# A first norm completed ahead of the projections, whose products are convolved and gated from PSUM in pairs of banks

## The chip, the cores and the metric

One NeuronCore of a Trainium2 chip runs one program. The metric is the device time of one execution in microseconds. TensorE (PE) multiplies matrices into PSUM, eight banks of 512 float32 columns on 128 partitions. The DVE (VectorE) and ACT (ScalarE) read PSUM and SBUF, POOL (GpSimd) reads SBUF alone. DMAs are issued by SP's queue. Each engine works off its own list in order and waits on semaphores for the others.

## The reference, cut to what matters

The model has two layers, a Hyena mixer and a differential attention. The change lies in the first of them:

```python
y = rmsnorm(h, norm_pre[i])                     # y = h * rsqrt(mean(h*h) + 1e-6) * g
u = y @ w_in + b_in                             # 1024 -> 8192
streams = dwconv_centred(u[..., :3 * D_INNER], conv_w, conv_b)   # 3 taps along the tokens
x0, x1, v = jnp.split(streams, 3, axis=-1)
z = u[..., 3 * D_INNER:]
h_fwd, h_bwd = hyena_filters(T, ...)            # a small sine network over the positions
v = bidir_long_conv(v * x1, h_fwd, h_bwd, skip) # by FFT in the reference
y = v * x0
return (y * jax.nn.silu(z)) @ w_out
```

There are T = 528 tokens (16 meta tokens and 512), 1024 channels and 2048 inner channels.

## The kernel before

Everything is held transposed, channels on partitions and the 528 tokens along the free axis, so x is eight slabs of 128 x 528. For float32 accuracy each operand of a large matmul is split into a rounded high part and the rest (`hi` on ACT, line 209, and `lo`, line 212), and a product takes three matmuls: high by high, high by rest, rest by high (`project`, line 396). One output tile of a projection, 128 channels by 528 tokens, is 8 slabs x 3 products x 2 halves of 264 tokens, 48 matmuls, done in two steps of 24 (slabs 0 to 3, slabs 4 to 7).

There are 64 such tiles in Hyena: for each of eight chunks two tiles each of v, x, y and z (`in_items`, `in_tile`). The matmuls of the tiles are filler: a `Filler` holds them as a list of steps, each with a cost in microseconds, and the code of the stages asks it to put so many microseconds of steps between its own instructions (`run`, `upto`). `fetch` loads a weight tile and splits it. A scheduler then orders each engine's list by a simulated time line, with the order of the program as priority; an instruction can be given a higher priority (`high_priority`), a fixed order (`keep_in_program_order`), or an edge behind another on the same engine (`issue_after`).

In the kernel before, `first_load` loads x slab by slab, multiplies by the gain and splits it, and sums the squares on the DVE (line 511), while the projections begin at once with the gained but not yet normed x. `first_norm` takes the column sums by six matmuls (line 270), computes 1/rms by the DVE (`rsqrt`), and spreads it over the partitions into `rb0` (line 286, line 525). Since the norm is a factor of each token, it is applied when a product leaves PSUM: `scaled` in `in_tile` (line 554) multiplies each half, one bank, by `rb0` on the DVE into SBUF (`u`, or `cv` for z). From there a three-tap convolution is made of one ACT step (line 569, middle tap and bias) and two DVE steps (lines 570 and 571). GpSimd writes minus the bias into the two edge columns of `u` (line 566) so that the bias vanishes at the ends. For z, ACT takes silu (line 559).

The eight banks of PSUM are two pools: `psB` with five single banks and `psP` with three. Projected tiles take two banks of `psP` (one tile takes them from `psB`), as do the transforms of the filter's taps (`tap_transform`, lines 753 to 760); the output projection (`out_tile`, line 918) takes two banks of `psB`, each half added to the accumulator by the DVE (line 925).

The order of the stages: the sine network (`filter_net`, three layers, line 637) and the tables run with the first four tiles and four more steps, then `filters` makes the taps of eight chunks and transforms them with filler between, then eight times `long_conv` with the tiles of the next chunk and the output tiles of the last as filler, then `boundary` (second norm) and the attention. In `taps` the first product's row 0 is multiplied by one half (line 720).

## Time and profile before

| | |
|---|---|
| median of 3 runs | 1425.76 us (1424.94 to 1428.54) |
| the profiled execution | 1427.81 us |
| its span, first to last instruction | 1426.0 us |
| TensorE busy | 1339.9 us, 94% |
| DVE, ACT, GpSimd busy | 1094.9, 740.5, 569.0 us |
| mean granted TensorE clock | 0.977 |
| Hyena's share of the span | until about 705 us |

The profile is one execution on the chip. It has a page with sums, and a trace that can be asked for any stretch: busy times by window, instructions in order of time, what each idle time of an engine ended with. A row that ends with `[6.48 <-DVE sqk L280]` says that the engine stood idle for 6.48 us before it and that the DVE's instruction of line 280 on tile sqk ended that. TensorE's matmuls are pipelined and overlap in their rows; the distance of their starts tells their rate. One float32 matmul with a single column has two records. A few per cent of the matmul records can be missing.

### The profile page before, as it was taken

The page shows a single profiled execution, that of the slowest core. Times are in us where ns is not written, and L with a number is a line of the kernel's source. Part 1 is how long each engine was busy: PE and PEld are TensorE (multiplying, and loading weights), DVE is VectorE, ACT ScalarE, POOL GpSimd, SP SyncE. Part 2 cuts the span into 40 slices and gives each one's busy share as a digit, 9 for nine tenths or more (in the row PEclk, how much of TensorE's full clock was granted, in tenths as well). Part 3 has the DMA queues.
Part 4 walks back from the last instruction along what each step waited for, and adds up shares of the span by engine and source line. Part 5 has one row for each costly group of instructions (what it writes and reads, how often), then busy time and mean ns, then how long its engine had stood idle before and what let it go on. Part 6 is the DMA issues. An engine that isn't in the chain of part 4 may idle for free. (4 is left out here: it accounts for less than half of the span.)

```text
span 1426.0 us, 25213 instructions
## 1 busy us (share of the span) xinstructions
PE 1339.9 (94%) x9296; PEld 1245.4 (87%) x9296; DVE 1094.9 (77%) x1979; ACT 740.5 (52%) x1415; POOL 569.0 (40%) x671
## 2 busy tenths in 40 slices
PE   5889999999999999999989899999999999999995
PEld 4789889889899999999889788898898989898884
DVE  8889988888988888888877765675656676675677
ACT  5345533453535353534344767666555556666543
POOL 6266634432333323242432234434333343434325
PEclk9899999999999999999979899999999999999998
DMA  6244342668978686877431322323332231322341
GB/s 203 93 140 156 137 152 90 205 231 269 315 241 300 216 288 219 287 239 259 148 110 40 117 89 89 108 85 119 118 117 106 76 132 46 145 92 111 125 157 59
DMA packets 104171, 222.10 MB, mean 156 GB/s; under 512 B 11808, under 2 KB 16160, under 8 KB 104048
## 3 DMA queue, kind: packets, MB, share of 16 engines
q1 hardware_dynamic: 104048, 220.49, 44.6%
q8 instruction: 73, 1.20, 0.3%
q14 instruction: 50, 0.41, 0.1%
HBM read 158.58 MB, written 61.87 MB: 155 GB/s over the span
## 5 line engine op out<-in xcount | busy, mean ns | idle before, releaser
L396 PE MATMUL b<-xh,wh 128*128 128x264 f32 x1024 | 268.3, 293 | 13.9 <-DVE u L554 10.9
L396 PE MATMUL b<-xl,wh 128*128 128x264 f32 x1024 | 264.8, 290 | 2.6 <-DVE xl L506 2.6
L396 PE MATMUL b<-xh,wl 128*128 128x264 f32 x1024 | 262.2, 290 | 1.1 <-POOL wl L212 1.1
L396 PEld LDWEIGHTS b<-xh,wh 128*128 128x128 f32 x1024 | 185.3, 194 | 19.6 <-DVE u L554 13.7
L396 PEld LDWEIGHTS b<-xl,wh 128*128 128x128 f32 x1024 | 184.7, 194 | 4.8 <-DVE xl L506 3.5
L209 ACT CAST wh<-wr 128x512 fp32r<-128x512 f32 x220 | 129.7, 618 | 109.0 <-DMA wr<-in_w_in 33.9
L396 PEld LDWEIGHTS b<-xh,wl 128*128 128x128 f32 x1024 | 183.4, 193 | 1.9 <-POOL wl L212 1.4
L212 POOL TENSOR_TENSOR wl<-wr,wh 128x512 fp32r<-128x512 f32 x64 | 90.9, 1441 | 103.0 <-ACT wh L209 102.8
L212 DVE TENSOR_TENSOR wl<-wr,wh 128x512 fp32r<-128x512 f32 x156 | 123.5, 818 | 10.1 <-ACT wh L209 9.7
L353 ACT CAST ah<-ar 128x512 fp32r<-128x512 f32 x94 | 56.7, 617 | 88.2 <-DMA ar<-in_w_z 29.6
L1382 DVE TENSOR_REDUCE mx<-a 128x1 f32<-128x528 f32 x128 | 89.0, 697 | 15.2 <-PE a L1379 15.1
L393 PE MATMUL b<-xh,wh 128*128 128x512 f32 x232 | 92.8, 400 | 4.4 <-DVE acc L1325 4.4
L393 PE MATMUL b<-xl,wh 128*128 128x512 f32 x232 | 91.9, 396 | 0.0
L212 DVE TENSOR_TENSOR pl<-b,ph 128x512 fp32r<-128x512 f32 x64 | 43.9, 688 | 62.4 <-ACT ph L209 62.4
L393 PE MATMUL b<-xh,wl 128*128 128x512 f32 x232 | 91.7, 395 | 0.0
L566 POOL TENSOR_SCALAR u<-vecs 128x1 f32<-128x1 f32 x96 | 42.4, 460 | 123.5 <-DVE cv L571 73.6
L354 DVE TENSOR_TENSOR al<-ar,ah 128x512 fp32r<-128x512 f32 x94 | 70.1, 755 | 26.9 <-ACT ah L353 26.1
L1388 POOL COPY pp<-pp 128x80 f32<-128x80 f32 x64 | 20.8, 325 | 145.6 <-DVE pp L1387 105.0
L1325 DVE SCALAR_TENSOR_TENSOR acc<-b,rh,acc 128x512 f32<-128x512 f32 x96 | 70.4, 743 | 10.6 <-PE b L1310 10.4
L1262 PE MATMUL b<-wh,xh 128*128 128x256 f32 x256 | 74.1, 289 | 0.4 <-DVE vl L1272 0.4
L1262 PE MATMUL b<-wl,xh 128*128 128x256 f32 x256 | 73.0, 285 | 0.0
L1262 PE MATMUL b<-wh,xl 128*128 128x256 f32 x256 | 72.8, 284 | 0.0
(391 smaller groups left out, 4101.3 us busy)
## 6 DMA issues: line engine op xcount, KB each, us to landing
wr<-in_w_in SPq DMA_DIRECT2D x128, 256.0 KB, 3.8
hsp<-ho SPq DMA_DIRECT2D x16, 512.0 KB, 2.6
ar<-in_w_v SPq DMA_DIRECT2D x32, 256.0 KB, 4.2
wr<-in_w_out SPq DMA_DIRECT2D x32, 256.0 KB, 3.7
H<-hsp SPq DMA_DIRECT2D x16, 512.0 KB, 4.7
w_v_h<-ah SPq DMA_DIRECT2D x32, 256.0 KB, 3.3
w_v_l<-al SPq DMA_DIRECT2D x32, 256.0 KB, 3.4
ar<-in_w_out SPq DMA_DIRECT2D x32, 256.0 KB, 4.0
```

Of the source, the lines that this page charges most:

```text
L209: self.nc.scalar.copy(dst, src)
L212: (eng or self.nc.vector).tensor_tensor(dst, src, hi.bitcast(F32), op=ALU.subtract)
L353: keep(nc.scalar.copy(h, raw))
L354: keep(nc.vector.tensor_tensor(l, raw, h.bitcast(F32), op=ALU.subtract))
L393: te.matmul(ps, w[:, wk], x[:, k, first:T], start=st, stop=sp)
L396: te.matmul(ps[h], w[:, wk], x[:, k, h * TH:(h + 1) * TH], start=st, stop=sp)
L566: g.tensor_scalar(u[:, e:e + 1], b_in[:, mt:mt + 1], -1.0, None, op0=ALU.mult)
L1262: te.matmul(ps[:n, :256], x, wv[k // 4][w][:, wk], start=(k == 0 and q == 0), stop=(k == KT - 1 and q == len(ops) - 1))
L1325: self.nc.vector.scalar_tensor_tensor(y, ps, r, y, op0=ALU.mult, op1=ALU.add)
L1382: v.tensor_reduce(mx, ps[:, :, :TH], axis=AX.XY, op=ALU.max, negate=True)
L1388: self.nc.gpsimd.tensor_copy(view(p, 0, [META, 5], [1, META]), view(p, MR - META, [0, 5], [1, META]))
```

## The change

It completes the norm before the projections. `first_load` loads all of x first, with the network's table behind slab 1 and the vectors behind slab 5, then the first two weight tiles. Squares are summed by TensorE: six one-column matmuls a slab. `first_norm` has a shorter root (a power on GpSimd and one Newton step on the DVE), makes the row factors by six small matmuls (`rows`) and then multiplies each slab by gain and factor on the DVE, casts it on ACT and subtracts on the DVE, at high priority and in a fixed order. What follows on ACT and DVE is put behind the last slab.

`in_tile` no longer scales. ACT reads a pair of banks and writes the middle tap with bias into a padded buffer `cv` (six fixed ones), the DVE adds the left and right taps from the pair, shifted by writing at another offset, and GpSimd adds an edge correction to two columns, computed once. Silu of z is read from the pair as well. PSUM becomes `psB` with four single banks and `psP` with two pairs; output tiles take pairs, too, and are evacuated by one instruction. Items 1 and 2 of the first chunk's steps are exchanged, one layer of the network runs ahead of the norm instead of two, and with two steps after each later layer ten steps are asked for before the filters instead of eight. The factor one half goes into the constant `hbas`.

```diff
--- before.py
+++ after.py
...
     hbas = np.stack([np.cos(sg), np.sin(sg)]).transpose(3, 0, 1, 2, 4)
+    hbas[0, 0, 0, 0] *= 0.5
...
         px = ExitStack()
-        self.psB = px.enter_context(tc.tile_pool(name="ps0", bufs=5, space=PSUM))
-        self.psP = px.enter_context(tc.tile_pool(name="ps1", bufs=3, space=PSUM))
+        self.psB = px.enter_context(tc.tile_pool(name="ps0", bufs=4, space=PSUM))
+        self.psP = px.enter_context(tc.tile_pool(name="ps1", bufs=2, space=PSUM))
         with ExitStack() as cx:
...
             cb2 = self.tl(k0, [P, 48], F32, "cb2")
-            self.rb0 = self.tl(k0, [P, T], F32, "rb0")
+            edge = self.edge = self.tl(k0, [P, 48, 2], F32, "edge")
+            self.cv = [self.tl(pa, [P, T + 2], F32, f"cv{i}", bufs=1) for i in range(6)]
+            self.cv_at = 0
+            for t in self.cv:
+                g.memset(view(t, 0, [T + 1, 2]), 0.0)
...
             items += vx(0)
+            items[1], items[2] = items[2], items[1]
             for c in range(NCH):
...
                 with tc.tile_pool(name="pf", bufs=1) as pf:
-                    net = self.net_load(pf)
-                    part = self.first_load(pf, fill)
-                    self.load(dtl, I["dtail"])
+                    xts, sums, net = self.first_load(pf, fill)
+                    layers = self.filter_net(pf, hs, net)
+                    next(layers)
+                    with tc.high_priority(offset=400):
+                        last = self.first_norm(pf, xts, sums)
                     g.tensor_tensor(cb2, cw[:, 0], cw[:, 1], op=ALU.add)
...
                     g.tensor_tensor(cb2, cb2, cb, op=ALU.add)
-                    layers = self.filter_net(pf, hs, net)
-                    for _ in (0, 1):
-                        next(layers)
-                    self.first_norm(pf, self.rb0, part)
-                    fill.fetch(2, g)
-                    fill.upto(4)
-                    for _ in layers:
-                        fill.upto(fill.at + 2)
-                    self.tables(pf, vb, nb, ib, hb)
+                    for i in (0, 1):
+                        g.tensor_tensor(edge[:, :, i], cw[:, 2 * i], b_in[:, 0:48], op=ALU.mult)
+                    g.tensor_scalar(edge, edge, -1.0, None, op0=ALU.mult)
+                    self.load(dtl, I["dtail"])
+                    with tc.issue_after(last[0]), tc.issue_after(last[1]):
+                        fill.upto(4)
+                        for _ in layers:
+                            fill.upto(fill.at + 2)
+                        self.tables(pf, vb, nb, ib, hb)
                 self.filters(fpool("pl"), hs, hb, dtl, rnt, dpf, dpb, hsp, lambda us: fill.run(us, first[1]))
...
         nc = self.nc
-        part = []
+        sums = self.tl(self.psB, [P, 512], F32, "b")
+        xts = []
         for k in range(KT):
...
             self.load(xt, self.I["xT"][:, k])
-            if k == 0:
+            xts.append(xt)
+            if k == 1:
+                net = self.net_load(pf)
+            if k == 5:
                 self.load(self.vecs, self.I["vecs"])
-                fill.fetch(0, nc.gpsimd)
-            gain = self.gains[:, 0, k:k + 1]
-            nc.scalar.activation(self.xh[:, k], xt, AF.Copy, scale=gain)
-            nc.vector.scalar_tensor_tensor(self.xl[:, k], xt, gain, self.xh[:, k].bitcast(F32), op0=ALU.mult,
-                                           op1=ALU.subtract)
+        for i in (0, 1):
+            fill.fetch(i, nc.vector)
+        for k, xt in enumerate(xts):
             sq = self.tl(pf, [P, T], F32, "sqk", bufs=4)
             nc.scalar.activation(sq, xt, AF.Square)
-            if part:
-                nc.vector.tensor_tensor(part[0], part[0], sq, op=ALU.add)
-            else:
-                part.append(sq)
-            if k == 3:
-                fill.fetch(1, nc.gpsimd)
-        return part
-
-    def first_norm(self, pf, rb, part):
-
-        r = self.token_rms(part, [(j * 88, j * 88 + 88) for j in range(6)])
-        dg = self.diagonals(r, 0, 6, 88, self.tl(pf, [P, T], F32, "sqk", bufs=4))
+            for j in range(6):
+                nc.tensor.matmul(sums[:88, j:j + 1], sq[:, j * 88:j * 88 + 88], self.ones[:, 0:1],
+                                 start=k == 0 and j == 0, stop=k == KT - 1 and j == 5)
+        return xts, sums, net
+
+    def first_norm(self, pf, xts, sums):
+
+        v, s, m = self.nc.vector, self.nc.scalar, 88
+        a, y, q, r = [self.tl(self.small, [P, 8], F32, t)[:m, :6] for t in ("rs_a", "rs_y", "rs_q", "rms")]
+        v.tensor_scalar(a, sums[:m, 0:6], 1.0 / D, 1e-6, op0=ALU.mult, op1=ALU.add)
+        self.nc.gpsimd.tensor_tensor(y, a, self.mhalf[:m, :6], op=ALU.pow)
+        v.scalar_tensor_tensor(q, y, -0.5, y, op0=ALU.mult, op1=ALU.mult)
+        v.tensor_tensor(q, q, a, op=ALU.mult)
+        v.scalar_tensor_tensor(r, q, 1.5, y, op0=ALU.add, op1=ALU.mult)
+        rb = self.tl(pf, [P, T], F32, "rb0")
         for h in (0, 1):
             ps = self.tl(self.psB, [P, 512], F32, "b")
-            self.spread(dg[:, h * TH:(h + 1) * TH], ps[:, :TH])
-            self.nc.scalar.copy(rb[:, h * TH:(h + 1) * TH], ps[:, :TH])
+            self.rows(r, 3 * h, 3, m, ps[:, :TH])
+            s.copy(rb[:, h * TH:(h + 1) * TH], ps[:, :TH])
+        keep = self.tc.keep_in_program_order
+        for k in range(KT + 1):
+            if k < KT:
+                xt, xh = xts[k], self.xh[:, k]
+                keep(v.scalar_tensor_tensor(xt, xt, self.gains[:, 0, k:k + 1], rb, op0=ALU.mult, op1=ALU.mult))
+                cast = keep(s.copy(xh, xt))
+            if k:
+                low = keep(v.tensor_tensor(self.xl[:, k - 1], xts[k - 1], self.xh[:, k - 1].bitcast(F32), op=ALU.subtract))
+        return cast.ins, low.ins
...
         if part == 0:
-            res["ps"] = [self.tl(self.psB if (c, idx) == (0, 1) else self.psP, [P, 512], F32, "b")[:, :TH] for _ in (0, 1)]
-        ps = res["ps"]
-        self.project(ps, wt, 0, part)
+            res["ps", idx] = self.tl(self.psP, [P, 2, 512], F32, "b")
+        ps = res["ps", idx][:, :, :TH]
+        self.project((ps[:, 0], ps[:, 1]), wt, 0, part)
         if part == 0:
             return
-        r2 = lambda t: t.rearrange("p (h t) -> p h t", h=2)
-
-        def scaled(dst):
-            for h in (0, 1):
-                sl = slice(h * TH, (h + 1) * TH)
-                v.tensor_tensor(dst[:, sl], ps[h], self.rb0[:, sl], op=ALU.mult)
-
+        cv = self.cv[self.cv_at % 6]
+        self.cv_at += 1
+        at = lambda o: view(cv, o, [TH, 2], [1, TH])
+        y = cv[:, 1:T + 1]
         if kind == "z":
-            z = self.tl(pa, [P, T], F32, "cv", bufs=4)
-            scaled(z)
-            s.activation(z, z, AF.Silu, bias=b_in[:, mt:mt + 1])
+            s.activation(at(1), ps, AF.Silu, bias=b_in[:, mt:mt + 1])
             gt = self.tl(pa, [P, T], F32, "G", bufs=2)
-            g.tensor_tensor(gt, res["y", i], z, op=ALU.mult)
+            g.tensor_tensor(gt, res["y", i], y, op=ALU.mult)
             res["G", i] = gt
             return
-        u = self.tl(pa, [P, T + 2], F32, "u", bufs=2)
-        for e in (0, T + 1):
-            g.tensor_scalar(u[:, e:e + 1], b_in[:, mt:mt + 1], -1.0, None, op0=ALU.mult)
-        scaled(u[:, 1:T + 1])
-        y = self.tl(pa, [P, T], F32, "cv", bufs=4)
-        s.activation(y, u[:, 1:T + 1], AF.Identity, bias=cb2[:, mt:mt + 1], scale=cw[:, 1, mt:mt + 1])
-        v.scalar_tensor_tensor(y, u[:, 0:T], cw[:, 0, mt:mt + 1], y, op0=ALU.mult, op1=ALU.add)
-        v.scalar_tensor_tensor(y, u[:, 2:T + 2], cw[:, 2, mt:mt + 1], y, op0=ALU.mult, op1=ALU.add)
+        s.activation(at(1), ps, AF.Identity, bias=cb2[:, mt:mt + 1], scale=cw[:, 1, mt:mt + 1])
+        for o in (2, 0):
+            v.scalar_tensor_tensor(at(o), ps, cw[:, 2 - o, mt:mt + 1], at(o), op0=ALU.mult, op1=ALU.add)
+        ends = view(cv, 1, [T - 1, 2])
+        g.tensor_tensor(ends, ends, self.edge[:, mt], op=ALU.add)
         res[kind, i] = y
...
                 v.tensor_tensor(pm[0:1, 0], pm[0:1, 0], pm[0:1, 1], op=ALU.add)
-                v.tensor_scalar(pm[0:1, 0], pm[0:1, 0], 0.5, None, op0=ALU.mult)
             else:
...
         ho = self.tl(ph, [P, 4, 256], F32, "ho", bufs=2)
-        ps = [self.tl(self.psP, [P, 512], F32, "b") for _ in (0, 1)]
+        ps = self.tl(self.psP, [P, 2, 512], F32, "b")
         for a in (0, 1):
...
                     for (bh, mh) in ((0, 0), (0, 1), (1, 0)):
-                        nc.tensor.matmul(ps[par][:, a * 256:(a + 1) * 256],
+                        nc.tensor.matmul(ps[:, par, a * 256:(a + 1) * 256],
                                          hb[a][bh][:, par, st, jt * P:(jt + 1) * P],
...
                         i += 1
-        pv = lambda q: ps[q].rearrange("p (a b) -> p a b", a=2)
+        pv = lambda q: ps[:, q].rearrange("p (a b) -> p a b", a=2)
         s.copy(ho[:, 0::2], pv(0))
...
         gs = st["g"]
-        pss = [self.tl(self.psB, [P, 512], F32, "b")[:, :TH] for _ in (0, 1)]
+        pair = self.tl(self.psP, [P, 2, 512], F32, "b")[:, :, :TH]
+        pss = [pair[:, h] for h in (0, 1)]
         sls = [slice(0, TH), slice(TH, T)]
...
                                      start=(i == 0 and q == 0), stop=(i == 1 and q == 2))
-        for ps, sl in zip(pss, sls):
-            ya = self.yacc[:, dt, sl]
-            if c == 0:
-                nc.scalar.copy(ya, ps)
-            else:
-                nc.vector.tensor_tensor(ya, ya, ps, op=ALU.add)
+        ya = self.yacc[:, dt].rearrange("p (h t) -> p h t", h=2)
+        if c == 0:
+            nc.scalar.copy(ya, pair)
+        else:
+            nc.vector.tensor_tensor(ya, ya, pair, op=ALU.add)
         if dt in (2, 6):
...
         for k in range(KT):
-            tag, bufs = ("cv", 4) if k < 4 else ("u", 2) if k < 6 else ("G", 2)
-            xt = self.tl(pa, [P, T], F32, tag, bufs=bufs)
+            xt = self.cv[(self.cv_at + k) % 6][:, :T] if k < 6 else self.tl(pa, [P, T], F32, "G", bufs=2)
             self.load(xt, I["xT"][:, k])
...
```

## Rows read from the trace of the kernel before

**Rows 1.** page, part 1: busy us, share of the span, instructions

```profile
PE 1339.9 (94%) x9296; PEld 1245.4 (87%) x9296; DVE 1094.9 (77%) x1979; ACT 740.5 (52%) x1415; POOL 569.0 (40%) x671
```

**Rows 2.** busy time by window: length, then PE, PEld, DVE, ACT, POOL; PEclk, DMA share, GB/s

```profile
0.00:60.00 60.00, 38.95 (x196) 34.32 (x197) 48.10 (x74) 28.06 (x44) 31.08 (x34) 0.86 0.45 154
60.00:100.00 40.00, 34.95 (x258) 33.83 (x257) 32.64 (x52) 20.66 (x35) 23.45 (x25) 0.91 0.38 123
100.00:200.00 100.00, 92.19 (x717) 88.45 (x716) 91.68 (x143) 49.02 (x92) 63.63 (x61) 1.00 0.44 154
200.00:705.00 505.00, 490.19 (x3775) 475.79 (x3774) 435.74 (x852) 224.71 (x387) 170.90 (x187) 1.00 0.70 234
```

**Rows 3.** timeline of TensorE: start us, us, line, tiles, count, idle before

```profile
29.88 1.92 PE L270 MATMUL b<-ones,sqk 128*88 128x1 f32 x12 [5.17 <-DVE sqk L511]
...
43.03 2.13 PE L286 MATMUL b<-sqk,ones 88*128 88x264 f32 x4 [6.48 <-DVE sqk L280]
...
45.40 0.64 PE L396 MATMUL b<-xl,wh 128*128 128x264 f32 x2
45.84 0.64 PE L396 MATMUL b<-xh,wl 128*128 128x264 f32 x2
...
82.90 0.79 PE L753 MATMUL b<-pm,hb0h 128*128 128x256 f32 x2 [4.83 <-ACT pm L209]
```

**Rows 4.** the projections' line alone by window: PE and PEld busy (count), PEclk, DMA, GB/s

```profile
0.00:45.00 45.00, 17.64 (x73) 15.80 (x74) 0.86 0.54 184
45.00:60.00 15.00, 13.99 (x96) 13.77 (x96) 0.84 0.18 64
60.00:74.70 14.70, 14.70 (x122) 14.51 (x120) 1.00 0.46 149
```

**Rows 5.** waits of TensorE, 100 to 705 us: total us, times, longest

```profile
PE b L396 <- DVE u L554: 10.9, 10, 2.9
...
PE b L753 <- DVE u L554: 3.5, 3, 1.3
...
PE b L753 <- ACT acc L209: 1.9, 1, 1.9
...
PE b L918 <- DVE acc L925: 0.6, 2, 0.4
```

**Rows 6.** single lines, whole span: count, ns min/median/max, first and last start

```profile
L509 ACT ACTIVATE sqk<-xt x8: 626/642/643, 4.6 to 21.1; 128x528 f32<-128x528 f32 x8
...
L506 DVE SCALAR_TENSOR_TENSOR xl<-xt,vecs,xh x8: 751/760/1782, 7.1 to 20.8; 128x528 fp32r<-128x528 f32 x8
...
L511 DVE TENSOR_TENSOR sqk<-sqk,sqk x7: 690/1304/2861, 11.2 to 28.5; 128x528 f32<-128x528 f32 x7
...
L1454 POOL TENSOR_TENSOR rh<-vv,mhalf x15: 1017/1020/1050, 856.1 to 1394.0; 128x4 f32<-128x4 f32 x15
...
L554 DVE TENSOR_TENSOR u<-b,rb x96: 373/422/436, 44.7 to 691.7; 128x264 f32<-128x264 f32 x96
...
L569 ACT ACTIVATE cv<-u,cb,vecs x48: 815/829/840, 46.1 to 692.8; 128x528 f32<-128x528 f32 x48
...
L720 DVE TENSOR_SCALAR pm<-pm x8: 282/1182/1275, 81.0 to 187.0; 1x256 f32<-1x256 f32 x8
...
L1325 DVE SCALAR_TENSOR_TENSOR acc<-b,rh,acc x96: 730/742/751, 912.5 to 1370.4; 128x512 f32<-128x512 f32 x96
```

**Rows 7.** network's last layer among groups of TensorE, 0 to 60 us: busy us, mean ns

```profile
L637 PE MATMUL b<-hd,net 64*128 64x264 f32 x4 | 1.2, 408 | 0.0
```

**Rows 8.** timeline of the DVE: two convolution chains, first and last of eleven

```profile
143.63 0.76 DVE L554 TENSOR_TENSOR u<-b,rb 128x264 f32<-128x264 f32 x2
...
150.58 0.75 DVE L571 SCALAR_TENSOR_TENSOR cv<-u,vecs,cv 128x528 f32<-128x528 f32 x1
...
398.27 0.76 DVE L554 TENSOR_TENSOR u<-b,rb 128x264 f32<-128x264 f32 x2
...
404.43 0.75 DVE L571 SCALAR_TENSOR_TENSOR cv<-u,vecs,cv 128x528 f32<-128x528 f32 x1
```

4 lines of the change are left out of this document (2 added, 2 removed).

## The prediction

> **What bounds the kernel now.** I read the engine part of the page first: TensorE is busy 94% of the span [rows 1]. Then the busy time by stage: it is above 97% busy from 200 us to 705 us, but only 39 of 60 us at the beginning, 35 of 40 after that and 92 of 100 in the third stage [rows 2]. So up to 705 us TensorE stands still for 21.0, 5.1, 7.8 and 14.8 us, 48.7 us in all. The change touches nothing behind 705 us but the tiles into which the boundary loads x, so a gain can come from these 48.7 us and from matmuls that run at TensorE's lower level (1.2 GHz), and from nowhere else.
>
> The timeline of the beginning tells where they lie [rows 3]. Six column sums start at 29.88 after 5.17 us of waiting for the DVE's sum of squares; the row factors follow at 43.03, after 6.48 us more; only then can projected tiles leave PSUM. After that wait the projections run at 0.22 us each (two in 0.44 us, from 45.40 to 45.84), against 122 in 14.7 us, 0.1205 us each, at granted clock 1.00 [rows 4]. By 60 us 73 + 96 = 169 projection matmuls are recorded [rows 4], seven steps of 24. The last wait of the beginning is at 82.90: the first tap transform waits 4.83 us for the rounded taps [rows 3].
>
> From 100 us on the waits by releaser say what is left: 10.9 us of projections and 3.5 us of tap transforms wait for the DVE scaling of L554, which empties one of the three shared banks [rows 5].
>
> **Start.** Removed: eight DVE adds of squares, the ACT rounding with gain, the scaling of each product. Added: 48 column-sum matmuls instead of 6, a power on GpSimd, six row matmuls for two, and per slab of x one DVE multiply, an ACT cast, a DVE subtraction, all before the first projection. The first square starts at 4.6 us and takes 0.64 us [rows 6], so sums start at 5.2. Six sums take 1.92 us [rows 3]: eight sets take 15.4 us if all run at the lower level, and they end at 20.6; if the clock rises on the way, and x arrives as fast as the sums run, they could end at 15. I take 18. From there: the power takes 1.02 us [rows 6], with the four small DVE steps and the hand-offs I estimate 2.2 us (at least 1.0, the power alone; at most 11.2, what lies between the end of the present sums and 43.03 [rows 3], where the DVE works on the filter network in between). The row matmuls are nearest to L286 and L270, some 2 us [rows 3]; a copy of half a row is about half of L569's 0.83, 0.5 with its hand-off; the first slab then needs 0.76 (L506) and 0.64 us (L509) [rows 6]. The first projection starts at T0 = 18 + 2.2 + 2.0 + 0.5 + 1.4 = 24.1, bounds 21 and 28.
>
> After T0 the DVE sets the pace: 0.76 + 0.69 us (L506, L511) less their overlap, about 1.35 us a slab [rows 6], 10.7 us for eight. The exchanged order of items 1 and 2 lets two tiles use slabs 0 to 3 first: 24 matmuls at 0.22 are 5.3 us, the next 24, in part at the higher level, 3.5; the third step waits for slab 7 and ends at about T0 + 11.8, the fourth at T0 + 14.7. Three more steps at 2.9 us and two filter layers at 1.2 us (L637 [rows 7]) make seven steps at T0 + 25.7 = 49.8 where the kernel before has them at 60. That is -10.2 us, bounds -13.3 and -6.3.
>
> The fetches of the first two weight tiles are moved behind all of x on SP's queue; their halves are needed at T0 only, 14 us later. The network's table moves behind two slabs, a DMA that the sums do not need. The new ordering edges put the third tile's cast, its subtractions and filter layers 2 and 3 behind the last slab on ACT and DVE. The projections wait for that tile at T0 + 14.7; the DVE is free at T0 + 10.7 and needs two subtractions, so it is hidden with 2.6 us to spare. Without that cover every microsecond counts.
>
> **Start of the taps.** L720 goes (the factor one half moves into a constant): 1.18 us at the median, eight times [rows 6], on the chain before 82.90. And five tiles instead of four are asked for before the filters begin, so more projections stand ready while the taps are rounded. The 4.83 us [rows 3] could go altogether, with the 2.3 us that a restart at the lower level costs (96 projections and a layer take 15 us from 45 to 60 [rows 4], 12.7 at the higher level): -7.1; or nothing is gained, if the network, now late on the DVE, makes the taps late. I take -3.2: L720's 1.2 and 2.0 of the remaining 3.6, since hidden and not hidden seem equally likely.
>
> **Emptying PSUM.** Each v, x or y tile loses two scalings of 0.42 us (L554: 96 + 32 times, 54 us of DVE in all), and its ACT and DVE steps read PSUM instead. The trace shows no dearer read there: a three-operand step of 512 columns from PSUM takes 0.742 us (L1325), of 528 from SBUF 0.760 (L506) [rows 6], 1.449 and 1.439 ns a column. The Trainium skill, VectorE: DVE Perf Modes, § Rules for kernel authors, says to copy a matmul's output to SBUF first if many operations will read it. By these rows the copy would cost 0.84 us a tile and win nothing in the operations themselves.
>
> What is lost is the early release. Today a bank is free after its scaling; afterwards the pair is held until the last of three steps. I followed all 48 such tiles from the start of the second scaling (0.34 us behind the first, where one row holds both) to the end of L571: eleven took longer than the 48 x 0.1205 = 5.8 us that the next tile covers, the first 7.4 us (from 143.97), the last 6.6 (from 398.61) [rows 8], together 18 us too long. Less the scaling itself 13.7 us. Against that, two pairs instead of three banks let a whole tile run while the other is emptied. So the 14.4 us of L554 [rows 5] go, and 0 to 14 come; I take 6, as the freed DVE shortens the queue and long-convolution matmuls often lie between. Net -8.4, bounds -14.4 and -0.4.
>
> **Smaller terms.** One tile less of projections is left to cover the transforms. At the end of that stage the transforms wait 1.9 us for rounded taps [rows 5]; I add as much, +1.9, bounds 0 and 5.8 (a whole uncovered tile). Output tiles take turns on two pairs with the projections; 12 matmuls cover 1.45 us, the add on the DVE remains the same work. Two waits of 0.3 us are there now [rows 5]: +1, bounds 0 and 12 (all 40 such tiles wait 0.3). GpSimd loses 96 small writes (L566), for which no wait of TensorE stands in [rows 5], and gets 48 edge sums, ahead of its own products: nothing, bounds -1 and +1. The boundary's loads go to the oldest tiles: nothing, same bounds.
>
> **Sum.** -10.2 - 3.2 - 8.4 + 1.9 + 1.0 = -18.9 us. Against the profiled execution (1427.8 us, span 1426.0) that gives 1408.9; the median of the three runs shown is 1425.8, 2 us less, which would give 1406.9. I say 1408.
>
> **Rivals.** *The norm stays as slow as now*: the chain from the sums to the factors takes its 11 us again because DVE steps of layer 1 and of the first weight tiles lie between. T0 becomes 18 + 11.2 + 2.0 + 0.5 + 1.4 = 33, the start gains 1 instead of 10, and 1427.8 - 18.9 + 9 = 1418. For it: exactly this happened between 31.8 and 43.03. Against it: priority 400, and no big GpSimd work beside it (L511, which now runs beside GpSimd's subtractions, takes between 0.69 and 2.86 us [rows 6]).
>
> *New waits equal the old ones*: the wait for a scaling becomes a wait for the convolution, 14 us instead of 6, and output tiles cost 4: 1427.8 - 18.9 + 8 + 3 = 1420.
>
> *The pair is held too long (slower)*: the convolution's two DVE steps stay at the end of a full DVE queue, as in the eleven chains, but for three quarters of the 48 tiles, and each exceeds its cover by the eleven's mean, 18.3/11 - 0.42 = 1.24 us: 36 x 1.24 = 45 us, instead of the 6 in the sum: 1448. It becomes slower than before from 25 us of such waits on, 20 tiles. The Trainium skill, PSUM — Partial Sum Buffer, § Summary: rules for kernel authors, speaks for this one: evacuate promptly. No row shows a pair held so; the eleven chains show that it is possible, the 37 others that it is not the rule.
>
> *It doesn't do what it says*: the scheduler puts the projections ahead of the norm as it likes. Data dependence excludes it: the first matmul reads the normed slab.
>
> **Chances.** Forecast 0.72, slow norm 0.11, waits that merely change their name 0.10, held pairs 0.07. A measurement here can tell about 0.3%, 4.3 us, from no change: 1421.5 is the bound. The forecast and about half of the second and third (their spread is some 5 us) are faster: 0.82; the rest of these 0.11 within; slower 0.07. Range: the forecast's own ends, all bounds together, are 1392 and above 1420; leaving one in ten on each side I give 1393 to 1424.
>
> **What would show it.** Right: the first projection between 21 and 28 us and no gap over 2 us after it up to 60; fewer than 7 us of TensorE waits on the convolution's DVE line; DVE busy about 50 us less. Wrong: TensorE waits for the second convolution step for over 20 us; sums that end after 22 us; a gap before the first transform as long as now or longer.

## The result, and the profile after

The changed kernel takes 1435.84 us (median of 4 runs, 1435.44 to 1438.92), beside 1425.96 us for the kernel before (4 runs, 1424.94 to 1428.54): a ratio of 1.0071, 95% interval 1.0052 to 1.0091. The forecast was 1408, with a range from 1393 to 1424. The change makes the kernel slower by 10 us where 18 us less were expected.

The engine part of the page of the changed kernel, in the columns of [rows 1]:

```profile
span 1437.1 us, 25180 instructions
...
PE 1355.7 (94%) x9388; PEld 1261.7 (88%) x9388; DVE 1030.8 (72%) x1801; ACT 735.7 (51%) x1407; POOL 526.0 (37%) x627
```

The DVE has 64 us less to do, more than the 50 that were forecast. TensorE's share is what it was. Busy time by window, in the columns of [rows 2], of the changed kernel:

```profile
0.00:60.00 60.00, 46.74 (x297) 43.30 (x298) 42.01 (x64) 28.16 (x44) 21.18 (x32) 0.94 0.46 157
60.00:100.00 40.00, 37.42 (x267) 35.91 (x267) 30.60 (x44) 19.01 (x32) 19.37 (x20) 0.91 0.41 129
100.00:200.00 100.00, 92.12 (x692) 88.80 (x692) 81.61 (x127) 50.46 (x95) 62.43 (x58) 0.97 0.44 146
200.00:260.00 60.00, 50.44 (x339) 46.83 (x338) 43.38 (x93) 20.15 (x35) 18.08 (x19) 0.89 0.28 94
260.00:705.00 445.00, 433.45 (x3336) 421.75 (x3335) 338.45 (x599) 193.66 (x334) 123.71 (x132) 0.99 0.76 250
```

and of the kernel before, for the last two stretches:

```profile
200.00:260.00 60.00, 59.09 (x458) 57.26 (x457) 52.12 (x114) 23.77 (x40) 25.10 (x26) 1.00 0.29 98
260.00:705.00 445.00, 431.09 (x3318) 418.53 (x3318) 383.62 (x739) 200.93 (x348) 145.80 (x161) 1.00 0.75 252
```

The first two stretches are fuller than in [rows 2]. In the first that is not yet a gain: the new column sums take 14.4 us of it instead of 1.9, and 177 projection matmuls are recorded in it against 168. From 200 to 260 us TensorE works 50.4 us instead of 59.1, and at granted clock 0.89. The waits of TensorE up to 740 us (total us, times, longest):

```profile
PE b L397 <- DVE cv L583: 10.7, 3, 6.8
PE b L932 <- DVE acc L938: 7.8, 7, 2.7
PE b L932 <- ACT gh L210: 5.9, 1, 5.9
PE b L521 <- ACT sqk L519: 4.1, 1, 4.1
```

L397 is the projections' line, L583 the second convolution step, L932 the output tiles' line, L938 their sum into `yacc`. The longest two stand in TensorE's timeline (start us, us, line, tiles, count, idle before):

```profile
40.22 0.40 PE L397 MATMUL b<-xh,wl 128*128 128x264 f32 x2
47.39 0.78 PE L397 MATMUL b<-xh,wh 128*128 128x264 f32 x2 [6.77 <-DVE cv L583]
47.96 0.65 PE L397 MATMUL b<-xl,wh 128*128 128x264 f32 x2
...
237.93 0.66 PE L867 MATMUL b<-ibh,Zl 128*128 128x272 f32 x4
244.51 1.25 PE L932 MATMUL b<-gh,wh 128*128 128x264 f32 x4 [5.92 <-ACT gh L210]
246.84 0.81 PE L932 MATMUL b<-gl,wh 128*128 128x264 f32 x2 [1.08 <-DVE gl L213]
```

At 40.2 both pairs are full and neither is emptied until 47. At 238 the inverse transforms of chunk 0 end and the next entry of TensorE's list is an output tile, whose gated values do not exist yet. In the kernel before, projections go on at that place, with one gap of 0.3 us:

```profile
238.57 0.29 PE L854 MATMUL b<-ibh,Zl 128*128 128x272 f32 x1
238.70 0.29 PE L396 MATMUL b<-xh,wh 128*128 128x264 f32 x1
...
249.55 0.28 PE L396 MATMUL b<-xl,wh 128*128 128x264 f32 x1
```

**Seven milestones** tell more than sums of waits, because every kernel here passes them. The times are starts, read from the rows of the timelines (of hs: its end): the 168th projection matmul; the filter network's result hs; the first tap matmul (weights w4h); the last matmul of the tap transforms (L753 before); the last inverse matmul of chunk 0 and of chunk 2; the first column sum of the boundary's norm.

| kernel | 168th proj. | hs | first tap | last transform | chunk 0 | chunk 2 | boundary | span |
|---|---|---|---|---|---|---|---|---|
| before | 59.9 | 68.5 | 74.8 | 196.9 | 238.6 | 334.4 | 722.8 | 1426.0 |
| changed | 58.9 | 69.9 | 75.6 | 198.0 | 238.3 | 345.6 | 734.4 | 1437.1 |
| e1 | 59.3 | 69.6 | 75.9 | 198.9 | 241.3 | 334.2 | 746.6 | 1449.4 |
| e2 | 59.4 | 69.0 | 76.0 | 198.7 | 241.0 | 335.8 | 728.6 | 1430.4 |
| e3 | 52.9 | 76.9 | 84.1 | 205.6 | 244.1 | 338.8 | 730.9 | 1436.6 |
| e4 | 53.6 | 70.4 | 78.3 | 201.6 | 242.0 | 348.0 | 735.8 | 1438.6 |
| e5 | 59.0 | 69.1 | 75.6 | 198.5 | 240.8 | 333.7 | 721.7 | 1424.5 |
| e8 | 49.6 | 73.5 | 79.1 | 202.2 | 239.7 | 346.9 | 739.2 | 1441.7 |
| e8s | 49.9 | 73.4 | 79.2 | 202.8 | 241.8 | 341.6 | 725.9 | 1428.6 |
| e9 | 50.2 | 72.6 | 78.1 | 203.2 | 242.3 | 335.3 | 734.6 | 1437.8 |
| e10 | 58.3 | 59.7 | 68.6 | 195.5 | 234.8 | 342.8 | 728.9 | 1430.1 |
| e11 | 58.1 | 57.8 | 66.7 | 191.7 | 233.1 | 328.6 | 717.5 | 1420.6 |
| e12 | 57.2 | 57.8 | 66.7 | 192.4 | 233.8 | 326.2 | 716.9 | 1420.3 |
| e13 | 57.6 | 55.7 | 71.6 | 196.7 | 238.0 | 334.1 | 725.9 | 1428.8 |
| e14 | 51.4 | 61.8 | 67.8 | 192.8 | 234.0 | 329.7 | 716.8 | 1419.7 |

Of the 11.1 us by which the changed span is longer, nothing arises up to chunk 0 (-0.3), 11.5 us between the ends of chunks 0 and 2, 0.4 from there to the boundary, and -0.5 behind it. Against the sum of the forecast (-18.9, by the profiled execution) this is 30 us too much: some 11 up to chunk 0, where -10.2, -3.2 and +1.9 had been put, some 11 between chunks 0 and 2, and some 8 where the emptying was to gain. Each row of the table is one execution. Those of e5 and e14 lie 2 and 4 us under their medians, those of the changed kernel, e2, e3, e8s and e13 2 to 4 us above theirs, so verdicts go by the ratios below, and a difference of 3 us between two rows shows nothing by itself. One of the seven executions of e3 ran at a granted clock of 0.844, took 1491.19 us and is left out of its ratio.

### The profile page after: what moved, and what is told of

The parts are those of the page before. It is cut to its first block, busy times and chain, and to the rows that moved or that the text cites. A ratio compares the mean times of both kernels' runs of the same rounds, so it can differ in the third digit from the quotient of the medians.

```text
span 1437.1 us, 25180 instructions
## 1 busy us (share of the span) xinstructions
PE 1355.7 (94%) x9388; PEld 1261.7 (88%) x9388; DVE 1030.8 (72%) x1801; ACT 735.7 (51%) x1407; POOL 526.0 (37%) x627
## 5 line engine op out<-in xcount | busy, mean ns | idle before, releaser
L397 PE MATMUL b<-xh,wh 128*128 128x264 f32 x1024 | 213.1, 289 | 12.5 <-DVE cv L583 10.7
L397 PE MATMUL b<-xl,wh 128*128 128x264 f32 x1024 | 211.9, 288 | 0.0
L397 PE MATMUL b<-xh,wl 128*128 128x264 f32 x1024 | 209.7, 285 | 0.0
L397 PEld LDWEIGHTS b<-xh,wh 128*128 128x128 f32 x1024 | 160.8, 191 | 16.8 <-ACT vbh L210 6.9
L397 PEld LDWEIGHTS b<-xl,wh 128*128 128x128 f32 x1024 | 161.3, 190 | 0.3
L397 PEld LDWEIGHTS b<-xh,wl 128*128 128x128 f32 x1024 | 160.8, 190 | 0.6
L213 POOL TENSOR_TENSOR wl<-wr,wh 128x512 fp32r<-128x512 f32 x58 | 78.7, 1377 | 99.4 <-ACT wh L210 99.3
L355 DVE TENSOR_TENSOR al<-ar,ah 128x512 fp32r<-128x512 f32 x94 | 66.6, 722 | 54.0 <-ACT ah L354 53.6
L585 POOL TENSOR_TENSOR cv<-cv,edge 128x2 f32<-128x2 f32 x48 | 17.2, 358 | 197.5 <-DVE cv L583 185.5
L1337 DVE SCALAR_TENSOR_TENSOR acc<-b,rh,acc 128x512 f32<-128x512 f32 x96 | 70.4, 743 | 10.6 <-PE b L1322 10.4
L583 DVE SCALAR_TENSOR_TENSOR cv<-b,vecs,cv 128x528 f32<-128x528 f32 x96 | 73.1, 762 | 1.1
```

The lines of the kernel that those rows point to most:

```text
L213: (eng or self.nc.vector).tensor_tensor(dst, src, hi.bitcast(F32), op=ALU.subtract)
L355: keep(nc.vector.tensor_tensor(l, raw, h.bitcast(F32), op=ALU.subtract))
L397: te.matmul(ps[h], w[:, wk], x[:, k, h * TH:(h + 1) * TH], start=st, stop=sp)
L583: v.scalar_tensor_tensor(at(o), ps, cw[:, 2 - o, mt:mt + 1], at(o), op0=ALU.mult, op1=ALU.add)
L585: g.tensor_tensor(ends, ends, self.edge[:, mt], op=ALU.add)
L1337: self.nc.vector.scalar_tensor_tensor(y, ps, r, y, op0=ALU.mult, op1=ALU.add)
```

## The experiments

Times are medians; ratios are to the kernel before, run on the same chip. Edits are to the changed kernel unless another is named. Three theories are weighed in the first ones. *Turns*: output tiles now draw from the same two rotating pairs as the projections, so TensorE must take both kinds in the order of the list. *Hold*: a pair stays occupied through three steps of two engines. *Port*: DVE steps become longer beside GpSimd's subtractions.

**e1: the list.** In every chunk, v/x tiles of the next chunk ahead of the output tiles of the last.

```diff
                 items += yz(c)
-                if c > 0:
-                    items += whole(outs[c - 1])
                 if c + 1 < NCH:
                     items += vx(c + 1)
+                if c > 0:
+                    items += whole(outs[c - 1])
```

> One edit to the changed kernel: in the list of filler steps the v and x tiles of the next chunk stand ahead of the previous chunk's output tiles. PSUM and everything else as in the changed kernel. Theory A (turns): the two pairs are handed out in the order of the list, so the tiles behind the output tiles of chunk 0 cannot start before these have their gated values; then the wait of 5.9 us at 244 us of the changed kernel's trace and the lower level after it go, and the time falls by 9 to 13 us, to 1423 to 1427. Theory B (hold): TensorE stands still because each pair is held through three evacuating steps by a late DVE, whatever the order of the list; then the time stays within 3 us of 1436.

Measured: 1451.72 us, ratio 1.0165 (1.0123 to 1.0206). Chunk 2 ends at 334.2, as early as before: the wait at 244 us is gone. But from there to the boundary 412.4 us pass instead of 388.8:

```profile
PE b L397 <- DVE cv L583: 19.9, 10, 5.2
PE b L932 <- DVE acc L938: 14.6, 9, 3.2
...
PE b L932 <- DVE cv L583: 3.6, 4, 1.2
```

With shared pairs the order of the list decides what waits; the exchange with banks of their own was not run. Neither theory had a time as long as this.

**e2: banks of their own.** Output tiles in two single banks of the other pool, as in the kernel before; projections and tap transforms keep the pairs.

```diff
-        pair = self.tl(self.psP, [P, 2, 512], F32, "b")[:, :, :TH]
-        pss = [pair[:, h] for h in (0, 1)]
+        pss = [self.tl(self.psB, [P, 512], F32, "b")[:, :TH] for _ in (0, 1)]
...
```

The lines left out empty the two banks one by one, as in the kernel before.

> One edit to the changed kernel: output tiles take two single banks of the pool of four and are evacuated half by half, as in the kernel before; projections and tap transforms keep the two pairs. Theory A (turns): projections no longer stand behind output tiles, so the wait at 244 us goes as with the exchanged list, 1423 to 1428, with up to 4 us of new waits in the pool of four, which the long convolution needs too. Theory B (hold): the pairs are held as long as before, 1433 to 1437.

Measured: 1430.0 us, ratio 1.0023 (1.0004 to 1.0041). Chunk 2 ends at 335.8 instead of 345.6. The waits for the convolution stay, and grow:

```profile
PE b L397 <- DVE cv L583: 15.1, 10, 5.0
```

From the end of chunk 0 to that of chunk 2 94.8 us pass, where the changed kernel needs 107.3 and the kernel before 95.8. So turns, not hold, make the loss there.

**e3: the norm alone.** New norm and list; five and three single banks, the old emptying (with a plain copy in place of the scaling), old output tiles and boundary.

```diff
-        self.psB = px.enter_context(tc.tile_pool(name="ps0", bufs=4, space=PSUM))
-        self.psP = px.enter_context(tc.tile_pool(name="ps1", bufs=2, space=PSUM))
+        self.psB = px.enter_context(tc.tile_pool(name="ps0", bufs=5, space=PSUM))
+        self.psP = px.enter_context(tc.tile_pool(name="ps1", bufs=3, space=PSUM))
...
-                v.tensor_tensor(dst[:, sl], ps[h], self.rb0[:, sl], op=ALU.mult)
+                v.tensor_copy(dst[:, sl], ps[h])
```

> The new norm alone: the norm is complete before the projections and the list of steps is the changed kernel's, but PSUM (five single banks and three), the emptying by halves into SBUF (a plain DVE copy in place of the scaling), the convolution from SBUF, the edges, output tiles and boundary are the kernel before's. Theory A: without pairs no turn is lost at 244 us, and what the earlier start gained stays: 1418 to 1424. Theory B also gives 1418 to 1424, since nothing is held through three steps. If the start itself is the loss, it stays above 1430.

Measured: 1434.74 us, ratio 1.0042 (1.0019 to 1.0064). The 168th projection starts at 52.9, 7 us sooner than before, and the kernel is slower all the same: its first tap matmul starts at 84.1, 9.3 us later than before, and the boundary is reached 8.1 us later. A start that is 7 us ahead is worth nothing if the taps are late; e10 to e12 follow this up.

**e4: the tables later.** GpSimd's subtractions of the tables behind the second tile's edge sum.

```diff
...
-                        self.tables(pf, vb, nb, ib, hb)
+                        with tc.issue_after(self.edges[1]):
+                            self.tables(pf, vb, nb, ib, hb)
```

> One edit to the changed kernel: GpSimd's subtractions for the tables stand behind the edge sum of the second tile on GpSimd's list. Theory C (port): the wait of 6.8 us before the third tile at 47.4 us comes from DVE steps that are stretched while GpSimd subtracts (three weight subtractions in 4.07 us instead of 1.9, one scale step in 2.57 instead of 0.43, 4.3 us in all); then the wait falls to 1 to 3 us and the lower level after it may go, 4 to 6 us less, 1430 to 1432. Rival D (queue): the convolution is late because layer 2 and the weights stand ahead of it on the DVE; then the wait stays at 5 us or more and the time within 2 us of 1436.

Measured: 1441.29 us, ratio 1.0104 (1.0085 to 1.0123). The first wait falls from 6.77 to 2.16 us, and one of 4.49 comes 23 us later:

```profile
43.61 0.49 PE L397 MATMUL b<-xh,wh 128*128 128x264 f32 x2 [2.16 <-DVE cv L585]
...
67.14 0.78 PE L397 MATMUL b<-xh,wh 128*128 128x264 f32 x2 [4.49 <-DVE cv L585]
```

The three weight subtractions that took 4.07 us beside GpSimd's take 1.88 now. Port explains most of the wait at 47 us, but taking it away gains nothing: the first tap matmul is later, not sooner.

**e5: the list, once.** e1's exchange in chunk 1 alone (v/x tiles of chunk 2 ahead of chunk 0's output tiles).

> The changed kernel with one place of the filler list altered: only in chunk 1 the eight v/x tiles of chunk 2 stand ahead of the eight output tiles of chunk 0 (in the run that exchanged them in every chunk, new waits grew from 345 us on). Turns theory (output tiles now take their turn on the two shared pairs, so nothing behind them in the list can overtake them while they wait for chunk 0's gated values): the 5.9 us wait for the gated values at 244 us and the low clock behind it go, the later chunks stay as in the changed kernel, and the time falls by 5 to 10 us, to 1426 to 1431. Hold theory (the pairs are held through three emptying steps, and that is what the 10 us are): the sums of waits for L583 and L938 stay, the pieces just move, and the time stays within 3 us of the changed kernel, 1433 to 1439. If chunk 1's exchange only postpones the wait, there is a wait of 4 us or more for gated values somewhere between 256 and 345 us.

Measured: 1428.42 us, ratio 1.0016 (1.0001 to 1.0031). Chunk 2 ends at 333.7, the boundary is reached at 721.7, and from 200 to 350 us no wait is longer than 2.4 us. One exchange in the list takes back the whole loss of the shared pairs.

**e8, e8s, e9: the pair free after one step.** ScalarE copies the pair to SBUF and the three steps read the copy; on the changed kernel, on e2, and on e5.

```diff
+        u = self.tl(pa, [P, 2, TH], F32, "u", bufs=2)
+        s.copy(u, ps)
-        s.activation(at(1), ps, AF.Identity, bias=cb2[:, mt:mt + 1], scale=cw[:, 1, mt:mt + 1])
+        s.activation(at(1), u, AF.Identity, bias=cb2[:, mt:mt + 1], scale=cw[:, 1, mt:mt + 1])
         for o in (2, 0):
-            v.scalar_tensor_tensor(at(o), ps, cw[:, 2 - o, mt:mt + 1], at(o), op0=ALU.mult, op1=ALU.add)
+            v.scalar_tensor_tensor(at(o), u, cw[:, 2 - o, mt:mt + 1], at(o), op0=ALU.mult, op1=ALU.add)
```

> The changed kernel, but v, x and y tiles are first copied whole from the pair to SBUF by one ScalarE step, and the taps (one ScalarE, two VectorE steps) read the copy: the pair is held through one step instead of three, and ScalarE gets 48 steps of some 0.6 us more. Hold theory: PE's waits for L583, 10.7 us before 740 us with 6.8 of them at 47 us, go to under 2 us, waits for yacc (L938) fall too since VectorE is less often late for a pair that blocks the next, and the time falls by 8 to 12 us, to 1424 to 1428. Turns theory: only the waits at L583 go, the 5.9 us wait for the gated values at 244 us stays and stands at the head of the list, and most of what is gained before it is lost there: 1429 to 1434.

> Both at once: output tiles in two single banks, as in the kernel before (the run with this alone gave 1430.0 with 15.1 us of waits for L583), and the copy by ScalarE ahead of the taps. If turns and hold are two separate costs, both are gone: waits for L583 and the copy together under 3 us before 740 us, no wait of 4 us or more between 40 and 340 us, and 1414 to 1420, faster than the kernel before. If the time that hold waits take is only passed on (the gated values or the next weights are late instead), 1426 to 1430, no better than single banks alone.

> The copy ahead of the taps with the shared pairs kept and only chunk 1's order exchanged (v/x tiles of chunk 2 ahead of chunk 0's output tiles). If the turns cost only at chunk 0's gated values, this does the same as output tiles in single banks: within 4 us of that run, 1414 to 1424. If shared turns also cost at the later chunks (waits for L938, 7.8 us in the changed kernel), it stays 5 to 8 us above it.

Measured: e8 1442.96 us, ratio 1.0134 (1.0115 to 1.0152); e8s 1427.16, 1.0008 (0.9991 to 1.0024); e9 1439.48, 1.0122 (1.0089 to 1.0156). In e8 the wait at 47 us is gone and the 168th projection starts at 49.6, near the 49.8 of the forecast. By the ratios it is 9 us slower than the changed kernel nonetheless. TensorE then waits for the halves of the filter weights and of the taps, which ScalarE makes:

```profile
79.09 2.08 PE L726 MATMUL b<-w4h,hs 128*128 128x512 f32 x4 [3.33 <-ACT w4h L210]
...
88.06 0.58 PE L768 MATMUL b<-pm,hb0h 128*128 128x256 f32 x1 [4.30 <-ACT pm L210]
```

Little of that is left at the end of chunk 2, 1.3 us. Another 3.5 us come from there to the boundary, and 11 in e9 beside e5 (399.3 against 388.0), where the waits for the sums into `yacc` are 9.2 us against 7.8, and 11.2 against 5.5. How the copy makes these longer was not tried.

Beside e2, e8s has no wait for a convolution step left, and between chunk 0 and the boundary it is 3.5 us shorter (484.1 against 487.6), where e2's waits for these steps add up to 10.1 us. The 3.5 are the difference of two single executions and hold the copy's own price, and the two ratios' intervals overlap: hold seems to cost less here than its waits, and how much is open. As a price for shared pairs (e8, e9) the copy is a loss. e8 and e9 lie above all that was expected for them; e8s came out at its second case (1426 to 1430), in which the time of the waits is only passed on.

**e10, e11, e12: the second sine layer ahead of the norm.** The changed kernel issues only the first layer ahead of it. On the changed kernel, on e2 and on e5.

```diff
-                    next(layers)
+                    for _ in (0, 1):
+                        next(layers)
                     with tc.high_priority(offset=400):
                         last = self.first_norm(pf, xts, sums)
```

The expectations speak of a lead: how much sooner than in the kernel before the same amount of matmul work is done, counted from the records of the trace. As a few of these are missing, the milestones above replace it in what follows.

> The changed kernel with one step of the filter network moved: its second sine layer is issued ahead of the norm (as in the kernel before) and no longer behind it. What it is to tell: in the changed kernel the head start of 10.4 us at 40 us is gone by 100 us, and it is gone too where the first wait for a pair was taken away (the copy ahead of the taps: -10 at 50 us, +1.5 at 100 us). Network theory: the tap transforms start when the network's output hs is complete, 69.6 us against 68.2 us before, since VectorE does the second layer only behind the norm's sixteen steps; so TensorE's head start only brings projections forward that the later stretch lacks. Then with the layer moved hs is complete at 54 to 60 us, the tap transforms start at 56 to 64 us instead of 75.4, the lead over the kernel before at 230 us is 5 to 10 us instead of 0, and with the wait at 244 us left as it is the time is 1425 to 1431. Rival (the tap stretch is bound by its filler: what is not projected ahead is missing later, or the norm comes later by the layer's steps): hs comes earlier, the lead at 230 us stays within 3 us of zero, and the time stays 1432 to 1440.

> The second sine layer ahead of the norm, and output tiles in two single banks (1430.0 alone). Network theory: both losses are away, and the lead at 230 us (5 to 10 us) lasts to the end: 1418 to 1425, faster than the kernel before. Rival: 1427 to 1433, as single banks alone. Third possibility: the gap is closed before 230 us and opens at the first chunk instead, because what it needs (the transforms of the taps, tables) is not ready sooner: a wait of 4 us or more between 200 and 300 us and 1425 to 1431.

> The second sine layer ahead of the norm, shared pairs kept, and v/x tiles of chunk 2 ahead of chunk 0's output tiles (1428.4 alone). Network theory: 1416 to 1423. Rival: 1426 to 1431. If the lead makes the turns worse again (the list reaches chunk 0's output tiles sooner while the gated values come no sooner), a wait for gated values of 3 us or more stands between 235 and 280 us.

Measured: e10 1431.31 us, ratio 1.0019 (1.0003 to 1.0035); e11 1422.7, 0.9956 (0.9939 to 0.9973); e12 1423.4, 0.9962 (0.9943 to 0.9981). e11 and e12 are faster than both kernels. hs and the first tap matmul in the changed kernel and in e11 (count, ns min/median/max, first and last start):

```profile
L724 PE MATMUL b<-w4h,hs x4: 391/393/509, 75.6 to 76.4; 128*128 128x512 f32 x4
...
L213 DVE TENSOR_TENSOR hs<-hd,hs x1: 1610/1610/1610, 68.3 to 68.3; 64x528 fp32r<-64x528 f32 x1
```

```profile
L725 PE MATMUL b<-w4h,hs x7: 391/393/398, 66.7 to 84.2; 128*128 128x512 f32 x7
...
L213 DVE TENSOR_TENSOR hs<-hd,hs x1: 1724/1724/1724, 56.1 to 56.1; 64x528 fp32r<-64x528 f32 x1
```

Both come 12 and 9 us sooner, chunk 0 ends 5.2 us sooner than in the changed kernel and the boundary is reached 16.9 us sooner. The expected 56 to 64 us for the first tap matmul was too early: TensorE's fixed list still has 233 projection matmuls ahead of it (304 in the changed kernel, 288 before).

**e13, e14: the wait at 47 us once more**, on e11, now that the network is no longer last. e14: the copy for the first four v/x tiles only (`if c == 0 and idx < 4:`). e13: the tables behind the first tile's edge sum.

> The fastest kernel so far (second sine layer ahead of the norm, output tiles in single banks: 1422.7) with the copy ahead of the taps for the first four v/x tiles of chunk 0 alone. It asks whether the wait for a pair that every kernel here has at 46.8 us (4.7 us in that kernel, 6.8 in the changed one) costs its length now that the filter network is no longer what comes last. If so: the wait goes under 1 us (as it did with the copy for all tiles), the lead over the kernel before at 55 us of projections' work stays 9 us or more, and the time is 1417 to 1420. If the tap transforms take it back (they start when hs is complete, and ScalarE, which makes the copies, also makes hs and the weights' halves): the wait goes and the time stays 1421 to 1425, the lead at 230 us 7 to 10 us as without the copy. If ScalarE becomes the late one (3.3 us of waits for the filter weights' halves when all tiles were copied): 1425 to 1430.

> The same kernel (1422.7), with no copy, and the tables' halves made by GpSimd behind the first tile's edge sum: VectorE's steps at 40 to 46 us are no longer beside GpSimd's subtractions of 128x1024. Port theory of the wait at 46.8 us: VectorE's stretched steps there (2.51 us for one that takes 0.43 us elsewhere, 2.18 for one of 0.69) go back to 0.4 to 0.8 us, the wait falls from 4.7 to 1 to 2.5 us, hs is complete 2 to 4 us sooner (57.6 in that kernel), and, as the tables are then late for the first tap transform instead, the time is anything from 1418 to 1426. Hold theory (three steps by two engines, each behind others in its queue): the wait stays at 4 us or more with the steps at their short lengths.

Measured: e14 1425.21 us, ratio 0.9982 (0.9969 to 0.9996); e13 1427.65, 1.0008 (0.9995 to 1.0021). Neither is better than e11 (0.9956). In e14 TensorE's first projections run without a wait until 61 us, but then it waits where it had not in e11:

```profile
67.82 2.07 PE L729 MATMUL b<-w4h,hs 128*128 128x512 f32 x4 [3.73 <-ACT w4h L210]
...
80.32 0.43 PE L771 MATMUL b<-pm,hb0h 128*128 128x256 f32 x1 [3.42 <-ACT pm L210]
```

In e13 hs is complete 2.1 us sooner than in e11, and the first tap matmul comes 4.9 us later: the scheduler put 282 projection matmuls ahead of it instead of 233. In e13 the wait at 47 us is 2.1 us instead of 4.5, in e14 it is gone. Neither gained by it; but as both edits make something else late, they do not show that the wait costs nothing by itself.

## Why the prediction was wrong, point by point

**What bounds the kernel.** The forecast counted TensorE's idle time up to 705 us and took every idle microsecond at the start for one that could be won. That step failed first. Between the first tap matmul and the last of the tap transforms 121.5 to 126.9 us pass in every one of the fifteen kernels, and from there to the end of chunk 0 another 38 to 42. In each of them 576 projection matmuls stand ahead of that last one in TensorE's list, so what is projected early is missing later: 240 of the 576 are left for the stretch in e8 (123.1 us, granted clock 0.92), 343 in e11 (125.0 us, 0.99). Before the end of chunk 0, a change is therefore worth some two thirds of what it does to the start of the taps: from e11 to e3 this start moves by 17.4 us, the end of chunk 0 by 11.0. The changed kernel starts the taps 0.8 us later than the kernel before, e3 9.3 later, e11 8.1 sooner; the ends of chunk 0 are -0.3, +5.5 and -5.5. What sets the pace within the stretch was not tried.

**Start, -10.2.** The sums ended at 20.4, not 18:

```profile
L521 PE MATMUL b<-ones,sqk x96: 284/285/307, 4.1 to 20.1; 128*88 128x1 f32 x96
```

They took 14.4 us of TensorE, 1.8 for six, near the 1.92 of [rows 3], so the faster pace that the 18 half counted on did not come; and the network's first layer, 2.0 us, lies among them. The chain to the factors took the 2.2 us that were forecast (20.44 to 22.62), so the rival of a slow norm is out. The row matmuls took 2.8 instead of 2.0, and the first projection starts at 27.5 instead of 24.1, inside the bounds. The 96th projection matmul starts at 40.3 us, against 49.9 before: at that point 9.5 of the 10.2 us are there. At the 97th, 2.6 are left, and the 168th comes at 58.9 where 49.8 was forecast. The step that failed is the sentence on the new ordering edges: it counted what they do to the third tile's weights and found it hidden, and forgot the same queue's work for the first two tiles' pairs. The DVE's timeline there:

```profile
36.72 1.00 DVE L599 TENSOR_SCALAR sa<-b,net 64x264 f32<-64x264 f32 x2
37.65 4.07 DVE L213 TENSOR_TENSOR wl<-wr,wh 128x512 fp32r<-128x512 f32 x3
41.64 2.57 DVE L602 TENSOR_SCALAR sk<-sa 64x528 f32<-64x528 f32 x1
44.24 0.43 DVE L603 TENSOR_SCALAR sk<-sk 64x528 f32<-64x528 f32 x1
44.59 0.75 DVE L583 SCALAR_TENSOR_TENSOR cv<-b,vecs,cv 128x528 f32<-128x528 f32 x1
45.27 0.69 DVE L608 SCALAR_TENSOR_TENSOR sa<-sk,sa 64x528 f32<-64x528 f32 x1
45.89 0.68 DVE L213 TENSOR_TENSOR wl<-wr,wh 128x512 fp32r<-128x512 f32 x1
46.49 0.75 DVE L583 SCALAR_TENSOR_TENSOR cv<-b,vecs,cv 128x528 f32<-128x528 f32 x1
```

The first pair is read by ScalarE from 39.4, and its two DVE steps stand behind the second sine layer and three weight halves. e8, where the pair is free after one step, has the 168th at 49.6, but that this is the forecast's 49.8 is luck: its projections begin 3.6 us later than forecast, and the 168 take 21.9 us instead of 25.7, with none of the two filter layers (2.4 us) among them. And it was worth nothing.

**Start of the taps, -3.2.** Measured +0.8. "The network, now late on the DVE" stood in the forecast as the bound at which nothing is gained, with even odds. But the second layer's first DVE step moved from 25.3 to 36.7 us (first row of the DVE's timeline above), behind the norm's sixteen steps; in the kernel before it stands here:

```profile
25.30 0.54 DVE L585 TENSOR_SCALAR sa<-b,net 64x264 f32<-64x264 f32 x1
```

That was to be read from the diff: the loop over two layers became one call. The step was worth 7 to 10 us: e10 gives 7.4 us back (ratio 1.0071 to 1.0019), e11 beside e2 9.6 (1.0023 to 0.9956). That a layer of the network on the DVE decides is shown by these pairs; that the rest of the way to the first tap matmul is the scheduler's list rather than data follows from e11, where TensorE runs projections for the 8.9 us between hs and w4h with one wait of 0.3 us, and from e13.

**Output tiles, +1 with bounds 0 and 12.** This is the term that carries the sign. The forecast priced the turn-taking by the waits that are there now, 0.3 us for a tile. The price is not a wait for a bank, but that the list cannot be overtaken: before, the eight output tiles of chunk 0 stood in their own banks' queue while 86 and more projection matmuls ran from 238 us on; now they stand in the way. Chunk 0's gated values come no sooner (first rounding at 243.8 us, against 241.8 before), so TensorE stands still for 5.9 us, starts again with two matmuls in 0.44 us (247.45 to 247.89), the granted clock of the stretch is 0.89, and the projections are late for chunk 2. It came to 11.5 us between the ends of chunks 0 and 2. e2 takes 8.5 us of the way from chunk 0 to the boundary, e5 15.2; from chunk 0 to chunk 2 alone they need 94.8 and 92.9 us instead of 107.3.

**Emptying PSUM, -8.4.** From the end of chunk 0 to the boundary the kernel before needs 484.3 us; with the new emptying and output tiles in single banks it is 487.6 (e2) or 484.4 (e11), with the old emptying and the new norm 486.8 (e3). With shared pairs and one exchange it is 480.9 (e5) and 483.1 (e12). The difference to the kernel before is -3.4 to +3.3 us, no more than single executions differ: no run shows a gain of the 8.4. The count of waits was sound: the 14.4 us of [rows 5] went, and from 100 us on 3.9 us came for the convolution in the changed kernel and 5.7 in e11, where 6 were taken. What failed is the step from there to the sum. Others came in their place; TensorE's waits in e11, 100 to 705 us:

```profile
PE b L397 <- DVE cv L584: 5.7, 5, 2.4
PE b L804 <- DVE y L793: 3.7, 3, 1.9
PE b L767 <- DVE ho L774: 3.6, 3, 1.9
PE b L397 <- DVE ho L774: 1.2, 1, 1.2
```

TensorE waited 0.6 us for y (L779) and 0.9 for ho of the DVE in the kernel before; now it is 3.7 and 4.8. By the code, ho's subtraction is the last step to read the pair that a tap transform fills, so these 4.8 us are waits for a pair again. Why these steps are late on a DVE that has less to do was not tried, and stays open. The second rival (waits that change their name) had this right, at 0.10, though under other names than it gave.

**Held too long, the rival on the slow side.** It was to decide from 25 us of waits for the second convolution step; there were 10.7. None of the signs of being wrong came: the sums ended before 22 us, and the gap at the first transform fell from 4.83 us to 1.9, while the taps started no sooner. No sign looked at when the taps start. The kernel is slower by another mechanism, so the 0.07 was given to the wrong one, and the 0.82 for faster rested on a sum of which more than half lay in a stretch that the taps bound. The terms' own upper bounds (-6.3, 0, -0.4, +5.8, +12) add up to +11.1 us, 1439 by the profiled execution. The forecast called that "above 1420" and cut the range at 1424, which left out what came.

**The copy.** The Trainium skill, VectorE: DVE Perf Modes, § Rules for kernel authors, leaves the choice for a product: take the plain rate of a PSUM source, or copy it to SBUF first where many operations follow (the forecast named the second alone). Here three do; the copy was slower with shared pairs (1.0134 against 1.0071) and not to be told apart with single banks (1.0008 against 1.0023, intervals overlap).

**Smaller terms.** Edge sums, the boundary's loads and the missing factor one half: no wait of TensorE names them (longest for the rounded taps 1.9 us); -0.5 us behind the boundary. The tile less of cover, +1.9 in the sum, does not show: from the first tap matmul to the last transform 122.4 us pass, 122.1 before.

## What to carry to other kernels

Ask of an idle microsecond at the start what the next stage waits for before counting it: here the next stage began with a side chain on the DVE, and a faster main chain that was put ahead of it won nothing. When two producers are given one rotating pool, their order in the program becomes binding; look for the place where the one in front has no data yet, and price the work that used to overtake it. A wait's length is not its price: here removing 10 us of waits changed the ratio by 0.0015, within its interval, and moving one call by a few lines bought 7 us.

## What the chip showed that had not been expected

- DVE steps become several times longer beside GpSimd's subtractions of 128x1024. A step of 128x528 in e11, and the same step in e13, where these subtractions come later:

```profile
40.30 2.51 DVE L604 TENSOR_SCALAR sk<-sk 128x528 f32<-128x528 f32 x1
```

```profile
40.30 0.43 DVE L606 TENSOR_SCALAR sk<-sk 128x528 f32<-128x528 f32 x1
```

- Convolution steps that read PSUM kept their 0.75 us beside such subtractions (one in the changed kernel, at 48.38 us; two in e11, at 42.73 and 48.01). With the copy in SBUF as their input one took 2.91 us (e14, at 51.84), though the one before it, at 50.21, took 0.75. The Trainium skill, SBUF — State Buffer, § SBUF: two separate sides, says that DVE and GpSimd share one pair of ports, which an operation holds for its whole length, and that a DVE operation needs it with two inputs in SBUF or in certain fast modes. The rows of the convolution agree; that the step of 0.43 us runs in such a mode, no row shows. It speaks against copying in a stretch where GpSimd is busy.
- Reading PSUM in a three-operand step cost nothing extra: 0.762 us at the median for 528 columns (L583, 96 times), 0.760 for L506 [rows 6].
